# Weight and token sums on VectorE, squares on ScalarE, and another order of the first down tile

## The chip, the cores and the metric

The kernel runs on one core of a Trainium2 chip. The metric is the device time of one execution in microseconds (us), the median of the runs. Names of engines in the rows: PE is TensorE (PEld its weight loads), DVE is VectorE, ACT is ScalarE, POOL is GpSimd, SP is SyncE, which here only issues DMAs.

## What is computed

One layer of an encoder, for 2048 prompt tokens and 64 sample tokens: a token mixer (attention, a state space model, a short convolution) and then a feed-forward part. The change lies in the feed-forward part, with D = 1024 and D_FF = 4096:

```python
x += W_down relu(W_up rmsnorm(x))^2
```

## The kernel before

**Stages.** The mixer with its projections takes about the first half of the time. It writes the normalized tokens h, transposed, to DRAM (h_d) and x to x2_d. Then comes the up stage (`phase_up`), which forms f = relu(W_up h)^2 and writes it to f_d, and then the down stage (`phase_down`), which reads f_d back and adds W_down f to x.

**Splits.** All matmuls are made of reduced-precision f32 operands: a value is split into a high half (ScalarE, a copy to the type fp32r) and a low half (VectorE, the value less its high half), and a product takes three matmuls, high·high, high·low, low·high.

**Up stage.** The 2112 tokens come in 3 blocks of 704, and a block is two halves of 352 (TH). d_ff comes in 16 groups of 256 columns. A *pair* is one group with one block: 48 pairs, numbered n = 16·b + f. A pair is a 2×2×2 block product (256 columns, 1024 inputs, 704 tokens, each cut in two) done with seven block products in place of eight, in the manner of Strassen and Winograd. For this it needs four sums of weight blocks, t1 to t4, for every pair, and four sums of token blocks, s1 to s4, for every block of tokens. Each of the seven products is 12 matmuls of 128x352 (4 slices of the inputs × 3 of the splits), 84 a pair. They stand in the list ORDER and are numbered 0 to 6: 11·11, s1·t1, s2·t2, s4·22, s3·t3, 12·21, 22·t4 (tokens·weights).

- `load_h(b)` (L1555) loads the tokens of a block to two tiles hr, from the GpSimd queue for block 0, else from SP's. `load_w(n)` (L1561) loads the weights of a pair to wr, which has two buffers.
- `tokens(b)` (L1563) forms s1 (L1579), s2 (L1581), s3 (L1582, in place in hr) and s4 (L1589) on GpSimd and splits all seven operands (L1574 on ScalarE, L1575 on VectorE). The sums s1, s2, s4 lie in tiles st with two buffers. In the rows the split tiles are as (from sums) and a.
- `weights(n)` (L1600) forms t1 to t4 on GpSimd (L1606 to L1609) in the tile tt, which has one buffer, and splits the seven weight operands (L1613, L1614) to tiles ws with ten buffers. In the rows they are wt (from sums) and w.
- `pair(b, f)` (L1646) runs the products (matmuls at L1643) into three PSUM banks, pa (products 0, 2, 4, 6, one on top of the other), pd (1, 3) and pb (5). Between them ScalarE copies pa to c11 after product 0 (L1657), pd to c22 (L1660) and pa to c12 after product 2 (L1663). VectorE adds: c12 += pd (L1666), c22 += pa after product 4 (L1670), c11 += pb (L1674); c21 is the relu of pa after product 6, on ScalarE (L1678). A product that adds to pa has to wait for the copy or addition that reads pa before it. VectorE squares each of the four quarters, 128x352, with relu (L1653), and SP stores the tile sm of 128x4x352 (L1680).
- `late_rows` (L1617) makes the last 128 prompt tokens' h during the first pairs.

**Down stage.** For each of 8 groups of four weight tiles (load L1718, split L1722 and L1723) and each of 17 token tiles, `tile` (L1751) does the products (L106 to L108) into PSUM and adds them to x (L1765); `load_f` (L1728) and `split_f` (L1743, L1744) bring the rows of f.

**Order.** The engines are not fed in the order of the source: a scheduler orders each engine's instructions by what they depend on, and each engine then works through its own list in order, waiting where an operand or a buffer isn't ready.

## Time and profile before

| | us |
|---|---|
| median of three runs | 2852.26 (2850.14 to 2855.62) |
| profiled execution, its own time | 2861.32 |
| its span in the trace | 2859.6 |
| TensorE busy in the span | 2701.5 (94%) |
| VectorE | 1808.2 (63%) |
| ScalarE | 1123.2 (39%) |
| GpSimd | 740.6 (26%) |

Times in the trace are counted from the start of the span. Busy times include the tail of an instruction that overlaps the next: matmuls are pipelined, so a dozen of 2.08 us starts 1.9 us after the dozen before it. The last matmul of the stage ahead of the up stage ends at 1412.47 us, the up stage's last at 2119.62, and the down stage's first starts at 2128.41. The mean granted clock of TensorE in the span is 0.972 of full speed.

### The profile page before, as it was taken

To read this page: it belongs to the slowest core of one execution; us is meant where nothing else is said; L and a number is where in the kernel's file an instruction comes from. 1 tells how busy PE (TensorE), PEld (TensorE's weight loads), DVE (VectorE), ACT (ScalarE), POOL (GpSimd) and SP (SyncE) were. 2 spreads that over 40 slices of the span, in tenths; PEclk is the share of its full clock that TensorE was granted. 3 is DMA by queue.
4 is the path that set the end of the run, shared out by engine and by line. 5 is a ranking of instruction groups with operands and counts; after the bars stand their busy time and mean duration, and the time that the engine had idled before them with its cause. 6 is when DMAs were issued, how large, how long until landed. Compare 5 with 4: busy or idle time off the path is not lost.

```text
span 2859.6 us, 39208 instructions
## 1 busy us (share of the span) xinstructions
PE 2701.5 (94%) x14438; PEld 2344.2 (82%) x14438; DVE 1808.2 (63%) x3367; ACT 1123.2 (39%) x2239; POOL 740.6 (26%) x770
## 2 busy tenths in 40 slices
PE   7999999788789999999889989999989999999999
PEld 7999998655556776688689979989988888888887
DVE  7647478478455677577678888888864444434433
ACT  5424243155557678833343444444431111111110
POOL 2101014122742225422345454444410000000000
PEclk9999999889899999999999999999999999999999
DMA  7545555533644134375435344333454222222223
GB/s 221 181 120 161 159 126 176 103 82 83 105 78 116 46 93 125 103 212 168 161 127 162 135 140 138 126 120 130 135 189 155 76 81 76 68 58 76 52 71 121
DMA packets 365715, 347.14 MB, mean 121 GB/s; under 512 B 43342, under 2 KB 324254, under 8 KB 362542
## 3 DMA queue, kind: packets, MB, share of 16 engines
q1 hardware_dynamic: 362707, 335.53, 40.7%
q0 software_dynamic: 2816, 9.11, 1.0%
q8 instruction: 114, 1.87, 0.3%
q14 instruction: 78, 0.64, 0.1%
HBM read 237.05 MB, written 107.46 MB: 120 GB/s over the span
## 4 chain that ended last, share of the span: by engine, by line
PE 46%; DVE 2%; POOL 1%; issue 1%; ACT 0%; DMA 0%; SPq 0%; DVEq 0%; ACTq 0%; POOLq 0%
PE pa L1643 12%; PE pd L106 8%; PE pd L107 8%; PE pd L108 8%; PE pd L1643 6%; PE pb L1643 3%; PE pd L114 1%; PE pd L113 1%; DVE sm L1653 0%; DVE wt L1614 0%; POOL s L1589 0%; DVE as L1575 0%; DVE w L1614 0%; DMA fr<-f_d 0%; POOL tt L1607 0%
## 5 line engine op out<-in xcount | busy, mean ns | idle before, releaser
L1765 DVE TENSOR_TENSOR acc<-acc,pd 128x512 f32<-128x512 f32 x272 | 186.7, 686 | 419.5 <-PE pd L108 414.2
L106 PE MATMUL pd<-dw,fh 128*128 128x512 f32 x1024 | 398.9, 390 | 8.8 <-ACT dw L1722 8.8
L107 PE MATMUL pd<-dw,fh 128*128 128x512 f32 x1024 | 399.0, 390 | 0.0
L108 PE MATMUL pd<-dw,fl 128*128 128x512 f32 x1024 | 398.6, 389 | 0.0
L1743 ACT ACTIVATE fh<-fr 128x512 fp32r<-128x512 f32 x128 | 81.0, 633 | 547.5 <-PE pd L107 537.8
L1250 DVE TENSOR_TENSOR pl<-p,ph 128x512 fp32r<-128x512 f32 (+2 forms) x242 | 176.2, 744 | 117.8 <-ACT ph L1249 107.9
L1151 DVE TENSOR_REDUCE pm<-mx 128x1 f32<-128x512 f32 (+2 forms) x320 | 185.3, 606 | 78.5 <-PE mx L1146 52.5
L106 PEld LDWEIGHTS pd<-dw,fh 128*128 128x128 f32 x1024 | 192.5, 188 | 49.0 <-ACT dw L1722 9.1
L107 PEld LDWEIGHTS pd<-dw,fh 128*128 128x128 f32 x1024 | 192.5, 188 | 41.2 <-DVE dw L1723 1.4
L108 PEld LDWEIGHTS pd<-dw,fl 128*128 128x128 f32 x1024 | 192.4, 188 | 39.9
L1246 ACT ACTIVATE p<-st 128x512 f32<-128x512 f32 (+2 forms) x320 | 165.8, 545 | 96.4 <-PE st L1242 51.9
L1643 PE MATMUL pa<-as,wt 128*128 128x352 f32 x1152 | 201.0, 323 | 0.0
L1613 ACT ACTIVATE wt<-tt 128x512 fp32r<-128x512 f32 x192 | 121.1, 631 | 173.6 <-PE pb L1643 51.7
L1643 PEld LDWEIGHTS pa<-as,wt 128*128 128x128 f32 x1152 | 188.1, 190 | 1.0 <-ACT sm L1657 0.5
L1614 DVE TENSOR_TENSOR wt<-tt,wt 128x512 fp32r<-128x512 f32 x192 | 184.1, 960 | 7.0 <-ACT wt L1613 2.6
L1614 DVE TENSOR_TENSOR w<-wr,w 128x512 fp32r<-128x512 f32 x144 | 154.2, 1071 | 49.9 <-ACT w L1613 49.8
L106 PE MATMUL pq<-wh,xh 128*128 128x384 f32 (+1 forms) x512 | 179.9, 351 | 5.0 <-ACT xh L233 4.6
L108 PE MATMUL pq<-wh,xl 128*128 128x384 f32 (+1 forms) x512 | 174.8, 341 | 0.5 <-DVE xl L234 0.3
L1249 ACT ACTIVATE ph<-p 128x512 fp32r<-128x512 f32 (+2 forms) x320 | 174.1, 582 | 2.1
L107 PE MATMUL pq<-wl,xh 128*128 128x384 f32 (+1 forms) x512 | 174.7, 341 | 0.0
L1250 POOL TENSOR_TENSOR pl<-p,ph 128x512 fp32r<-128x512 f32 (+1 forms) x78 | 95.0, 1221 | 255.2 <-ACT ph L1249 183.2
L1606 POOL TENSOR_TENSOR tt<-wr 128x512 f32<-128x512 f32 x48 | 68.5, 1427 | 343.5 <-DVE wt L1614 324.8
(483 smaller groups left out, 6403.7 us busy)
## 6 DMA issues: line engine op xcount, KB each, us to landing
wr<-in_w_up_dram SPq DMA_DIRECT2D x46, 1024.0 KB
f_d<-sm SPq DMA_DIRECT2D x48, 704.0 KB
fr<-f_d SPq DMA_DIRECT2D x128, 256.0 KB
raw<-in_w_in_dram SPq DMA_DIRECT2D x51, 512.0 KB
dr<-in_w_down_dram SPq DMA_DIRECT2D x28, 512.0 KB
qk_d<-stgT SPq DMA_DIRECT2D x16, 768.0 KB
xt<-in_x_prompt_dram SPq DMA_DIRECT2D x16, 512.0 KB
ka<-qk_d SPq DMA_DIRECT2D x16, 512.0 KB
```

The source lines that it names most:

```text
L106: nc.tensor.matmul(out, lh, rh, start=first, stop=False)
L107: nc.tensor.matmul(out, lh, rl, start=False, stop=False)
L108: nc.tensor.matmul(out, ll, rh, start=False, stop=last)
L1151: nc.vector.tensor_reduce(pm[:, t, c:c + 1], p[:, :n], axis=AX.X, op=ALU.max)
L1246: nc.scalar.activation(p[:, c0:], st[:, c0:], AF.Exp)
L1249: nc.scalar.activation(ph[:, c0:], p[:, c0:], AF.Copy)
L1250: (nc.gpsimd if g.idle and j else nc.vector).tensor_tensor(pl[:, c0:], p[:, c0:], f32(ph)[:, c0:], op=ALU.subtract)
L1613: ac.activation(t[:, 0], src[nm], AF.Copy)
L1614: ve.tensor_tensor(t[:, 1], src[nm], f32(t)[:, 0], op=ALU.subtract)
L1643: nc.tensor.matmul(bank, w[:, x, k], a[:, y, k], start=first and k + j == 0, stop=k + j == 5, skip_group_check=not first)
L1743: nc.scalar.activation(h, r, AF.Copy)
L1765: nc.vector.tensor_tensor(a[:, o], a[:, o], p, op=ALU.add)
```

## The change

- **Token sums.** `sums(b)` is split off `tokens(b)`: s1, s2, s4 and s3 are formed on VectorE, and the tiles st have three buffers. It is stepped, one sum a product, from the pair f = 13 of the block before, in the source; the loads of the tokens are asked for at f = 10 in place of 12.
- **Weight sums.** t1 to t4 are formed on VectorE for every pair but the first, which stays on GpSimd. `load_w(1)` stands after the weights and tokens of pair 0.
- **Squares.** The four squares on VectorE go. In their place ScalarE does a relu over c12 and c22 together (128x704), a relu over c11 (128x352), and one square of the whole tile (128x1408), in place.
- **First down tile.** In the first of the tiles of the down stage both halves of the outputs are done for one weight tile before the next one; the splits of the first token tile stand behind two of the four weight splits in the source.

```diff
-    def tokens(b):
+    def sums(b):
         h0, h1 = hr[b]
         a11, a12, a21, a22 = h0[:, 0:4], h0[:, 4:8], h1[:, 0:4], h1[:, 4:8]
...
-            return up.tile([128, 4, TH], F32, tag="st", bufs=2, name=f"{nm}_{b}")
...
-        po.tensor_tensor(s1, a21, a22, op=ALU.add)
...
-        po.tensor_tensor(s2, s1, a11, op=ALU.subtract)
-        po.tensor_tensor(a21, a11, a21, op=ALU.subtract)
...
+        s1, s2, s4 = (up.tile([128, 4, TH], F32, tag="st", bufs=3, name=f"{x}_{b}") for x in ("s1", "s2", "s4"))
+        src[b] = {"11": a11, "s1": s1, "s2": s2, "s4": s4, "s3": a21, "12": a12, "22": a22}
+        ve.tensor_tensor(s1, a21, a22, op=ALU.add)
         yield
+        ve.tensor_tensor(s2, s1, a11, op=ALU.subtract)
         yield
-        po.tensor_tensor(s4, a12, s2, op=ALU.subtract)
+        ve.tensor_tensor(s4, a12, s2, op=ALU.subtract)
         yield
+        ve.tensor_tensor(a21, a11, a21, op=ALU.subtract)
         yield
+    def tokens(b):
+        for i, (nm, _) in enumerate(ORDER):
+            t = A[b, nm] = up.tile([128, 2, 4, TH], F32R, tag=f"a{i}", name=f"a{nm}_{b}")
+            ac.activation(t[:, 0], src[b][nm], AF.Copy)
+            ve.tensor_tensor(t[:, 1], src[b][nm], f32(t)[:, 0], op=ALU.subtract)
+            yield
...
-        po.tensor_tensor(t1, b12, b11, op=ALU.subtract)
...
+        eng = po if n == 0 else ve
+        eng.tensor_tensor(t1, b12, b11, op=ALU.subtract)
+        eng.tensor_tensor(t2, b22, t1, op=ALU.subtract)
+        eng.tensor_tensor(t3, b22, b12, op=ALU.subtract)
+        eng.tensor_tensor(t4, b21, t2, op=ALU.subtract)
...
-        def square(c):
-            ve.scalar_tensor_tensor(c, c, 0.0, c, op0=ALU.max, op1=ALU.mult)
...
         ac.activation(c21, pa, AF.Relu)
-        square(c21)
+        r = sm[:, 2:4]
+        ac.activation(r, r, AF.Relu)
+        ac.activation(c11, c11, AF.Relu)
+        ac.activation(sm, sm, AF.Square)
...
     load_h(0, nc.gpsimd)
+    for _ in sums(0):
+        pass
     load_w(0, nc.gpsimd)
-    load_w(1, nc.gpsimd)
     weights(0)
     for _ in tokens(0):
         pass
+    load_w(1, nc.gpsimd)
...
-            if b < 2 and f == NP2 - 4:
+            if b < 2 and f == NP2 - 6:
                 load_h(b + 1)
             if n + 1 < 3 * NP2:
                 weights(n + 1)
-            nxt = tokens(b + 1) if b < 2 and f == NP2 - 1 else iter(())
+            if b < 2 and f == NP2 - 3:
+                nxt = sums(b + 1)
+            if b < 2 and f == NP2 - 1:
+                nxt = tokens(b + 1)
             pair(b, f, lambda: next(nxt, None))
...
+        if q + t == 0:
+            for j in range(QF):
+                for hf in range(2):
+                    products(hf, j)
         for hf in range(2):
-            o = slice(hf * 512, hf * 512 + 512)
-            p = ps.tile([128, 512], F32, tag="dn", bufs=6, name=f"pd{q}_{t}_{hf}")
-            for j in range(QF):
...
+            p, o = pp[hf], slice(hf * 512, hf * 512 + 512)
+            if q + t:
+                for j in range(QF):
+                    products(hf, j)
```

How the lists of the engines change, at three places. A name like w22_12 is the weight operand 22 of pair 12; the last number of a name only tells tiles apart.

**ScalarE, from pair 11 to 12 before.** The relu of c21 of a pair stands between the weight splits for the pair after the next, and the copy of c11 of the next pair (L1657) three rows on.

```order
L1613 ACTIVATE w11_13_16899<-wr13_16758 128x512
L1613 ACTIVATE wt1_13_16902<-tt13_16894 128x512
L1678 ACTIVATE sm11_16789<-pa11_16786 128x352
L1613 ACTIVATE wt2_13_16905<-tt13_16894 128x512
L1613 ACTIVATE w22_13_16908<-wr13_16758 128x512
L1657 ACTIVATE sm12_16923<-pa12_16920 128x352
L1613 ACTIVATE wt3_13_16911<-tt13_16894 128x512
```

The same stretch one pair sooner, after the change. The three new instructions of pair 10 are L1661, L1662 and L1663; the copy of c11 of pair 11 is L1641.

```order
L1661 ACTIVATE sm10_16657<-sm10_16657 128x704
L1600 ACTIVATE wt1_12_16763<-tt12_16755 128x512
L1662 ACTIVATE sm10_16657<-sm10_16657 128x352
L1659 ACTIVATE sm10_16657<-pa10_16654 128x352
L1600 ACTIVATE wt2_12_16766<-tt12_16755 128x512
L1663 ACTIVATE sm10_16657<-sm10_16657 128x1408
L1600 ACTIVATE w22_12_16769<-wr12_16620 128x512
L1641 ACTIVATE sm11_16784<-pa11_16781 128x352
```

The square over 1408 columns now stands ahead of one weight split and of the copy of c11.

**VectorE, in pair 8 before.** sm8 is the output tile of pair 8; L1666 and L1670 are the additions to c12 and c22.

```order
L1614 TENSOR_TENSOR w22_9_16390<-wr9_16246,w22_9_16390 128x512
L1614 TENSOR_TENSOR wt3_9_16393<-tt9_16376,wt3_9_16393 128x512
L1614 TENSOR_TENSOR w21_9_16396<-wr9_16246,w21_9_16396 128x512
L1666 TENSOR_TENSOR sm8_16405<-pd8_16403,sm8_16405 128x352
L1653 SCALAR_TENSOR_TENSOR sm8_16405<-sm8_16405 128x352
L1614 TENSOR_TENSOR wt4_9_16399<-tt9_16376,wt4_9_16399 128x512
L1670 TENSOR_TENSOR sm8_16405<-pa8_16402,sm8_16405 128x352
```

The same stretch of VectorE after: L1569, L1571 and L1573 are s1, s2 and s4 of block 1, L1650 and L1653 the additions.

```order
L1601 TENSOR_TENSOR w22_9_16382<-wr9_16239,w22_9_16382 128x512
L1569 TENSOR_TENSOR s1_1_17051<-hr1_1_16623 128x1408
L1601 TENSOR_TENSOR wt3_9_16385<-tt9_16368,wt3_9_16385 128x512
L1571 TENSOR_TENSOR s2_1_17052<-s1_1_17051,hr1_0_16622 128x1408
L1601 TENSOR_TENSOR w21_9_16388<-wr9_16239,w21_9_16388 128x512
L1650 TENSOR_TENSOR sm8_16397<-pd8_16395,sm8_16397 128x352
L1601 TENSOR_TENSOR wt4_9_16391<-tt9_16368,wt4_9_16391 128x512
L1573 TENSOR_TENSOR s4_1_17053<-hr1_0_16622,s2_1_17052 128x1408
L1653 TENSOR_TENSOR sm8_16397<-pa8_16394,sm8_16397 128x352
```

The scheduler has put three sums of block 1, whose pairs start with 16, into pair 8, ahead of its addition to c22; the first waits for the loads of hr1_1. The squares are gone.

**GpSimd, at the start of the up stage before.** The first rows are the loads of the weights of pair 1 and the sums of pair 0.

```order
L1561 DMA wr1_15264<-in_w_up_dram 128x8x256
L1606 TENSOR_TENSOR tt0_15266<-wr0_15262 128x512
L1608 TENSOR_TENSOR tt0_15266<-wr0_15262 128x512
L1607 TENSOR_TENSOR tt0_15266<-wr0_15262,tt0_15266 128x512
L1579 TENSOR_TENSOR s1_0_15292<-hr0_1_15257 128x1408
L1609 TENSOR_TENSOR tt0_15266<-wr0_15262,tt0_15266 128x512
L1581 TENSOR_TENSOR s2_0_15294<-s1_0_15292,hr0_0_15256 128x1408
L1582 TENSOR_TENSOR hr0_1_15257<-hr0_0_15256,hr0_1_15257 128x1408
```

After, from the load of the weights of pair 0:

```order
L1561 DMA wr0_15269<-in_w_up_dram 128x8x256
L1561 DMA wr1_15318<-in_w_up_dram 128x8x256
L1593 TENSOR_TENSOR tt0_15271<-wr0_15269 128x512
L1595 TENSOR_TENSOR tt0_15271<-wr0_15269 128x512
L1594 TENSOR_TENSOR tt0_15271<-wr0_15269,tt0_15271 128x512
L1596 TENSOR_TENSOR tt0_15271<-wr0_15269,tt0_15271 128x512
```

The load for pair 1 still stands ahead of the four sums of pair 0, though the source has it behind them; before it waited for nothing late, after it waits for VectorE's and TensorE's last use of a buffer of the stage ahead. The token sums are no longer in this list.

## Rows read from the trace of the kernel before

**Rows 1.** Busy time by stretch: us, then busy (instructions) by engine, PEclk, DMA share, GB/s

```profile
1412.47:2119.62 707.15, 659.47 (x4041) 655.29 (x4040) 580.22 (x699) 311.93 (x555) 332.46 (x204) 0.96 0.39 132
1412.47:1457.71 45.24, 23.82 (x107) 22.28 (x107) 31.58 (x35) 21.62 (x33) 27.48 (x12) 0.74 0.29 93
1915.00:2119.00 204.00, 204.00 (x1286) 203.89 (x1285) 163.19 (x210) 85.67 (x159) 86.11 (x60) 1.00 0.39 131
```

**Rows 2.** Waits from 1400 to 2125: us in total, times, longest

```profile
POOL tt L1606 <- DVE wt L1614: 324.8, 44, 13.6
...
PE pa L1643 <- DVE sm L1670: 27.7, 5, 7.1
```

**Rows 3.** Timeline of PE: start, us, group [idle before <-releaser]

```profile
1445.17 0.95 PE L1643 MATMUL pb<-a,w 128*128 128x352 f32 x2 [6.02 <-ACT w L1613]
...
1548.72 2.08 PE L1643 MATMUL pa<-a,w 128*128 128x352 f32 x12
...
1565.99 3.89 PE L1643 MATMUL pa<-a,wt 128*128 128x352 f32 x12 [5.58 <-DVE sm L1670]
1569.67 3.11 PE L1643 MATMUL pa<-a,w 128*128 128x352 f32 x12
...
1673.42 3.89 PE L1643 MATMUL pa<-a,wt 128*128 128x352 f32 x12 [7.07 <-DVE sm L1670]
...
1705.61 3.48 PE L1643 MATMUL pa<-a,wt 128*128 128x352 f32 x12 [6.61 <-DVE sm L1670]
...
1905.07 3.89 PE L1643 MATMUL pa<-a,wt 128*128 128x352 f32 x12 [6.99 <-DVE sm L1670]
```

**Rows 4.** Timeline of POOL, at the start, in pair 8, at the first block seam

```profile
1412.24 1.26 POOL L1609 TENSOR_TENSOR tt<-wr,tt 128x512 f32<-128x512 f32 x1
...
1416.59 4.55 POOL L1582 TENSOR_TENSOR hr<-hr,hr 128x1408 f32<-128x1408 f32 x1
...
1554.72 3.23 POOL L1579 TENSOR_TENSOR s<-hr 128x1408 f32<-128x1408 f32 x1 [3.66 <-DMA hr<-h_d]
...
1561.52 3.43 POOL L1582 TENSOR_TENSOR hr<-hr,hr 128x1408 f32<-128x1408 f32 x1
...
1659.10 5.74 POOL L1589 TENSOR_TENSOR s<-hr,s 128x1408 f32<-128x1408 f32 x1 [5.94 <-DVE as L1575]
```

**Rows 5.** Timeline of DVE, at the same three places

```profile
1414.50 9.66 DVE L1575 TENSOR_TENSOR a<-hr,a 128x1408 fp32r<-128x1408 f32 x3 [2.11 <-ACT a L1574]
...
1443.07 1.62 DVE L1575 TENSOR_TENSOR as<-s,as 128x1408 fp32r<-128x1408 f32 x1 [9.49 <-ACT as L1574]
1444.62 1.29 DVE L1614 TENSOR_TENSOR wt<-tt,wt 128x512 fp32r<-128x512 f32 x2
...
1553.43 0.69 DVE L1614 TENSOR_TENSOR wt<-tt,wt 128x512 fp32r<-128x512 f32 x1 [0.18 <-ACT wt L1613]
...
1561.87 3.63 DVE L1614 TENSOR_TENSOR wt<-tt,wt 128x512 fp32r<-128x512 f32 x1
...
1666.29 2.52 DVE L1575 TENSOR_TENSOR as<-s,as 128x1408 fp32r<-128x1408 f32 x1 [4.09 <-ACT as L1574]
```

**Rows 6.** Groups by shape, 1400 to 2125: count | busy us, mean ns | idle before

```profile
L1614 DVE TENSOR_TENSOR wt<-tt,wt 128x512 fp32r<-128x512 f32 x192 | 184.1, 960 | 7.0 <-ACT wt L1613 2.6
...
L1653 DVE SCALAR_TENSOR_TENSOR sm<-sm 128x352 f32<-128x352 f32 x192 | 152.2, 794 | 7.1 <-ACT sm L1678 2.6
L1613 ACT ACTIVATE wt<-tt 128x512 fp32r<-128x512 f32 x192 | 121.1, 631 | 173.6 <-PE pb L1643 51.7 <-issue 44.0 <-PE pd L1643 38.9
...
L1670 DVE TENSOR_TENSOR sm<-pa,sm 128x352 f32<-128x352 f32 x48 | 25.1, 523 | 7.5 <-PE pa L1643 7.3
...
L1574 ACT ACTIVATE as<-s 128x1408 fp32r<-128x1408 f32 x9 | 12.3, 1372 | 15.4 <-POOL s L1589 15.4
```

**Rows 7.** Timeline of ACT: the copy of c11 in pair 8

```profile
1551.38 0.45 ACT L1657 ACTIVATE sm<-pa 128x352 f32<-128x352 f32 x1
```

**Rows 8.** Timeline of DVE: the last square of the up stage

```profile
2120.14 0.53 DVE L1653 SCALAR_TENSOR_TENSOR sm<-sm 128x352 f32<-128x352 f32 x1 [1.32 <-ACT sm L1678]
```

More of the change, by code (lines that the diff above doesn't have):

```diff
@@ L1666, in pair @@
         ve.tensor_tensor(c12, pd, c12, op=ALU.add)
-        square(c12)
         product(b, n, 4, pa, False)
@@ L1670, in pair @@
         ve.tensor_tensor(c22, pa, c22, op=ALU.add)
-        square(c22)
         product(b, n, 5, pb, True)
@@ L1674, in pair @@
         ve.tensor_tensor(c11, pb, c11, op=ALU.add)
-        square(c11)
         product(b, n, 6, pa, False)
@@ L1688, in phase_up @@
         pass
+    load_w(1, nc.gpsimd)
     late = late_rows()
     NP2 = NF // 2
+    nxt = iter(())
     for b in range(3):
@@ L1755, in tile, with products @@
         last = q == NF // QF - 1
-        for hf in range(2):
-            o = slice(hf * 512, hf * 512 + 512)
-            p = ps.tile([128, 512], F32, tag="dn", bufs=6, name=f"pd{q}_{t}_{hf}")
-            for j in range(QF):
-                w = wts[q * QF + j]
-                if t < 16:
-                    mm3(nc, p, h[:, j], l[:, j], w[:, 0, o], w[:, 1, o], j == 0, j == QF - 1)
-                else:
-                    mm2(nc, p, h[:, j], w[:, 0, o], w[:, 1, o], j == 0, j == QF - 1)
+        pp = [ps.tile([128, 512], F32, tag="dn", bufs=6, name=f"pd{q}_{t}_{hf}") for hf in range(2)]
+        def products(hf, j):
+            p, w, o = pp[hf], wts[q * QF + j], slice(hf * 512, hf * 512 + 512)
+            if t < 16:
+                mm3(nc, p, h[:, j], l[:, j], w[:, 0, o], w[:, 1, o], j == 0, j == QF - 1)
+            else:
+                mm2(nc, p, h[:, j], w[:, 0, o], w[:, 1, o], j == 0, j == QF - 1)
+        if q + t == 0:
+            for j in range(QF):
+                for hf in range(2):
+                    products(hf, j)
+        for hf in range(2):
+            p, o = pp[hf], slice(hf * 512, hf * 512 + 512)
+            if q + t:
+                for j in range(QF):
+                    products(hf, j)
             nc.vector.tensor_tensor(a[:, o], a[:, o], p, op=ALU.add)
@@ L1778, in phase_down @@
         load_w(f, nc.gpsimd)
-    for f in range(QF):
+    for f in range(2):
         split_w(f)
-    for i in range(3):
-        load_f(*work[i])
+    load_f(*work[0])
+    split_f(*work[0])
+    for f in range(2, QF):
+        split_w(f)
+    load_f(*work[1])
+    load_f(*work[2])
     load_x(0)
     load_x(1)
-    split_f(*work[0])
     for i, (q, t) in enumerate(work):
```

27 lines of the change are left out of this document (2 added, 25 removed).

## The prediction

> **What bounds the kernel now.** Start with the stages. The up stage runs from the last matmul of the stage before it, at 1412.47 us, to the end of its own last matmul at 2119.62: 707.15 us, in which TensorE is busy 659.47 us at a mean granted clock of 0.96 [rows 1]. Undisturbed, as in its last 204 us, TensorE has no gap at all, the clock is 1.00, and a matmul takes 204.00 / 1286 = 0.1586 us [rows 1]. The stage has 48 pairs × 84 = 4032 matmuls, which is 639.5 us at that pace. So 67.6 us are lost, and nothing that leaves the matmuls alone can gain more here. A pair takes 84 × 0.1586 = 13.3 us.
>
> Where are they lost? The waits say that after the first pairs TensorE waits for one thing only: the addition at L1670 (c22) on VectorE, 27.7 us in 5 waits [rows 2]; product 6 of a pair may add to pa only after that addition has read it. The timeline has the four long ones: 5.58, 7.07, 6.61 and 6.99 us, **26.25 us** in all [rows 3]. After each the engine runs slower. At 1565.99 the granted clock has dropped and the next two dozens take 3.89 and 3.11 us instead of 2.08, which is 2.84 us more; the first dozens after the others take 3.89, 3.48 and 3.89, so 1.81 + 1.40 + 1.81 more [rows 3]. The **clock** costs at least 7.9 us; I take 8. The **start** is the rest: up to 1457.71, 45.24 us go by for 107 matmuls, which are worth 17.0 us [rows 1], so 28.3 us are lost there. 26.25 + 8 + 28.3 = 62.5 of the 67.6.
>
> Why is the addition late? At 1565.99 and 1705.61 it is GpSimd's three token sums, back to back (3.23 to 3.43 us each), and a low-half split beside them on VectorE takes 3.63 us where it takes 0.69 alone [rows 4, 5]. At 1673.42 and 1905.07, the block seams, it is s4: it has to wait 5.94 us for a buffer, since st has two, and takes 5.74 us; ScalarE and then VectorE wait for it, VectorE 4.09 us, with the addition queued behind [rows 4, 5].
>
> **The change, part by part.**
>
> *Weight sums from GpSimd to VectorE.* Before, a pair costs VectorE seven low halves at about 0.96 us, four squares at 0.79 and three additions at 0.52: 11.5 of 13.3 us [rows 6]. The first two means are swollen by GpSimd's work beside them; alone a half takes 0.69 [rows 5]. After it, seven halves and four sums at 0.69 and three additions at 0.52 make 9.2 us. In the middle of the stage this is worth nothing, since TensorE doesn't wait there; it makes the room for what follows. GpSimd itself waits 324.8 us for VectorE [rows 2], so its removal frees nothing by itself.
>
> *Squares from VectorE to ScalarE.* ScalarE gets a relu over 704 columns, one over 352 and a square over 1408 a pair. Nearest row: L1574, 128x1408, 1.372 us, against 0.631 for 512 [rows 6]; that is 0.83 ns a column, so 0.79 + 0.50 + 1.37 = 2.7 us. With 7 × 0.63 + 4 × 0.46 = 6.3 before, ScalarE is then busy 9.0 of 13.3 us. What counts is the order: the square stands ahead of one weight split and the copy of c11, which must have read pa before product 2 writes it, two products (3.81 us) into the pair. Before, the copy ends 2.66 + 0.45 = 3.11 us after the pair's first matmul [rows 3, 7]; laid out by its order with these durations it ends at about 3.4 us. Some 0.4 us is left, so the cost is nothing; if the square took twice as long it would not be (rival D).
>
> *Token sums ahead of their block, on VectorE, st with three buffers.* This removes GpSimd's back-to-back sums and the wait at the seam: 26.25 us of stalls and 8 of clock go. It adds three waits. VectorE is now the engine that waits for the tokens of block 1: s1 stands in pair 8, behind the fourth split for pair 9. There, GpSimd waited 3.66 us for the same transfer, which was in at 1554.72, 6.0 us after the pair's start at 1548.72 [rows 3, 4]. From 6.0, VectorE does s1, a split, s2, a split, the c12 addition, a split, s4 and the c22 addition: 3 × 1.54 + 3 × 0.60 + 2 × 0.5 = 7.4, so c22 is ready at 13.4 us and product 6 wanted it at 11.4 (6 × 1.905): a stall of **2.0 us**, 0 if the transfer comes 2 us sooner. Block 2 has the same in pair 17; its transfers are issued after other work of the seam, and I put 0 to 3 us there, value 1.2. The clock after these: 0.1 to 2.8 us each, value 0.7. At the two seams I lay out VectorE's list with 1.54 us for each of the splits, and c22 comes 0.2 us ahead of its need; 0 to 2 us in all, value 0.5.
>
> *The start.* VectorE's list from 1414.50 becomes: seven large operations (three splits, four sums), seven weight halves, four large splits. In a row one large operation starts 1.55 us after another and two halves take 1.29 [rows 5], so 1.54 and 0.60 us each, and the list ends at 1435.7. But GpSimd's four sums for pair 0 now run beside it: the next load of weights stands before them in GpSimd's queue, and it waits for the buffer that the stage before frees at its end. What such a company costs is seen at the same place before: three splits took 9.66 us instead of 4.8, while GpSimd did its own [rows 4, 5]. Four sums at 1.26 us [rows 4] in between give 1440.8. TensorE then has some 74 matmuls done about 6 us later, after low-clock dozens, so its lost time is 17.7 to 22.7 us instead of 28.3. What went: VectorE's wait of 9.49 us for s4 through ScalarE at 1443.07 [rows 5], and with it TensorE's wait of 6.02 us at 1445.17 [rows 3]. Gain 5.6 to 10.6, value **7**.
> The Trainium skill ("SBUF — State Buffer", section "SBUF: two separate sides") has GpSimd and a VectorE operation with two SBUF inputs exclude each other for a whole instruction. By that rule the start is the late end, a gain of 5.6, and without it 10.6; the trace agrees, 9.66 us for three splits, and so I stay near the late one.
>
> *First down tile.* TensorE takes the weight tiles in the order in which they are split; the other engines keep their order there. Worth 0.4 us at most, as a few of the tile's matmuls are left behind the last split. The last square of the stage now takes 1.37 instead of 0.53 us [rows 6, 8] ahead of its store and of the loads that TensorE waits for: +0.8. Together +0.4.
>
> **The sum.** 26.25 + 8 + 7 = 41.2 gained; 2.0 + 1.2 + 1.4 + 0.5 + 0.4 = 5.5 given back: 35.7. The profiled execution took 2861.3 us, so 2825.6; it stood 9.1 us above the median of 2852.26, and on the median it is 2816.6. I say **2816**.
>
> **The rivals.**
> A, the forecast, 2808 to 2824. For it: each stall has one cause in the rows, and the change removes each cause.
> B, *the wait moves to VectorE*: the transfers of tokens land late, VectorE stands with its whole list behind s1, and the stalls of pairs 8 and 17 are 5 us each with 2 us of clock. 14 instead of 4.6 given back: about 2826. For it: GpSimd did wait for this transfer; against: it never waited over 3.7 us.
> C, *the start gains nothing*, because it is as long with GpSimd's late sums: 2824. For it: the first stage of VectorE's list has grown from three to seven large operations; against: the 9.49 us behind s4 are gone for certain.
> D, *ScalarE is late for c11*. In-place Square over 1408 columns has no row; its floor is 1.37 us, and were it twice that, the copy of c11 would end at 4.8 instead of 3.4 and TensorE would wait 1.0 us in 46 pairs: 46 us, a time of 2862, slower than before. It decides from 0.78 us a pair (35.7 / 46); below that it only eats the gain, and 0.2 us a pair gives 2825. For it: no row shows this operation, the slack is only 0.4 us, and it is asked for 46 times; against: ScalarE's rows, 352, 512 and 1408 columns, lie on one line of 0.83 ns a column [rows 6, 7].
> The Trainium skill ("ScalarE: Activation LUTs", section "Rules for kernel authors") speaks against this part: relu and multiplications belong on VectorE. Its case is a faster bf16 mode; here in f32 the rows have 1.372 us for 1408 columns on ScalarE and 0.53 for 352 on VectorE, so it would cost some 0.6 us of an engine's spare time a pair, and no run here shows more.
> E, *the change does nothing*, because TensorE bounds the steady pairs anyway: within 5 us of 2852. Against it: the stalls are in the rows.
>
> **How the numbers follow.** A 0.66, B 0.13, C 0.11, D 0.07 (0.03 of it slower than before, 0.01 within 0.2%), E 0.03. The range reaches from A's good end, with all new waits at nothing (2816 - 5 - 4 = 2807, and 2 for what my 62.5 leaves out), to B with C and the small D: **2805 to 2832**. A difference of 0.2%, 5.7 us, is about what can be told from no change: faster 0.94, within 0.2% 0.03, slower 0.03.
>
> **What would show it.** After: no wait of TensorE for the c22 addition above 3 us; granted clock at or near 1.00 from 1460 to the end of the stage, and the stage about 671 us long. Low halves at 0.69 us on the mean. A wait of VectorE for the transfer of hr in pairs 8 and 17. The lost time of the start near 21 us. It is wrong if TensorE waits in every pair for the copy of c11 (D), or if the start still takes 28 us (C).

## The result, and the profile after

The changed kernel takes **2813.63 us** (median of 4 runs, 2809.31 to 2824.33), the kernel before, on the same chip, 2853.94 (4 runs, 2850.14 to 2865.24). The ratio is 0.9858, with an interval of 0.9817 to 0.9899, so 40 us less, 29 to 52. It was forecast at 2816, with a range of 2805 to 2832. The profiled execution took 2809.31 us.

Read the stages first. These are busy times by stretch of the kernel after; columns as in [rows 1]: us, busy (instructions) of PE, PEld, DVE, ACT, POOL, then PEclk, DMA share, GB/s. The rows are the up stage, its first 45.24 us (as long a stretch as the one in [rows 1]), its middle without the start, 460 us of that without any wait, and last the stage with the gap to the first matmul of the down stage.

```profile
1394.42:2065.68 671.26, 654.88 (x4041) 651.67 (x4040) 460.17 (x709) 418.08 (x698) 8.73 (x9) 0.99 0.42 140
1394.42:1439.66 45.24, 30.38 (x168) 29.15 (x168) 41.46 (x50) 29.42 (x47) 6.56 (x5) 0.81 0.46 145
1440.00:2060.00 620.00, 618.48 (x3839) 616.78 (x3838) 415.89 (x657) 387.08 (x649) 2.17 (x4) 1.00 0.42 141
1600.00:2060.00 460.00, 460.00 (x2853) 459.10 (x2853) 309.04 (x484) 290.80 (x483) 2.17 (x4) 1.00 0.41 138
1394.42:2075.28 680.86, 654.90 (x4041) 651.67 (x4040) 461.57 (x712) 422.17 (x704) 8.73 (x9) 0.98 0.42 142
```

The up stage is 707.15 - 671.26 = 35.9 us shorter, and 35.1 with the gap behind it, which was 715.94 - 707.15 = 8.8 and is 9.6. The granted clock is 1.00 behind the start. The spans differ by 2859.6 - 2807.6 = 52.0 us; of this 1412.47 - 1394.42 = 18.1 lie ahead of the up stage, where both kernels have the same code. That part is not counted to the change: in the fourteen profiles of this study that stage ends between 1394 and 1429 us, and for the kernels that were profiled twice at 1394 and 1405, at 1408 and 1409, at 1403 and 1414. (Of the 1429, 7.55 us do belong to an edit; they are told under *token sums back on GpSimd*.) One of its waits shows why. TensorE's matmuls of L1078 wait for tiles loaded from the key cache, for this long in all between 600 and 1000 us (us, times, longest), after:

```profile
PE sa_pk L1078 <- DMA sa_y<-in_cache_k_dram: 2.9, 2, 2.7
```

In the kernel before it was 13.8 us, and 9.7 when the changed kernel was profiled a second time. So single spans are not compared below; **U** is, the time from the last matmul ahead of the up stage to the first of the down stage: 715.94 before, 680.86 after.

The waits from 1400 to 2085 us, after (us in total, times, longest):

```profile
PE pa L1630 <- ACT w L1600: 11.7, 1, 11.7
...
PE pa L1630 <- DVE sm L1653: 1.5, 1, 1.5
...
DVE s L1569 <- DMA hr<-h_d: 2.2, 1, 2.2
```

Against [rows 2], TensorE's 27.7 us in 5 waits for the addition to c22 (now L1653) are down to a single 1.5. The timeline of PE shows it in its place (start, us, group, idle before):

```profile
1521.98 2.07 PE L1630 MATMUL pa<-a,w 128*128 128x352 f32 x12
...
1535.27 2.19 PE L1630 MATMUL pa<-a,wt 128*128 128x352 f32 x12 [1.52 <-DVE sm L1653]
1537.30 1.94 PE L1630 MATMUL pa<-a,w 128*128 128x352 f32 x11
```

1521.98 is the start of pair 8. The work behind the wait isn't slow, 2.19 us for a dozen where [rows 3] had 3.89 and 3.11: this short wait cost no clock. VectorE's timeline has the reason for the wait, and the state of the start:

```profile
1396.45 6.11 DVE L1583 TENSOR_TENSOR a<-hr,a 128x1408 fp32r<-128x1408 f32 x2 [2.12 <-ACT a L1582]
...
1527.84 1.62 DVE L1569 TENSOR_TENSOR s<-hr 128x1408 f32<-128x1408 f32 x1 [2.17 <-DMA hr<-h_d]
...
1533.16 1.62 DVE L1573 TENSOR_TENSOR s<-hr,s 128x1408 f32<-128x1408 f32 x1
1534.69 0.52 DVE L1653 TENSOR_TENSOR sm<-pa,sm 128x352 f32<-128x352 f32 x1
```

VectorE stood 2.17 us for the tokens of block 1 in front of s1; the addition came right behind s4. At the start two splits took 6.11 us beside GpSimd's weight sums. These stood behind the load of wr1 in GpSimd's list, which waited for TensorE's last use of the buffer in the stage ahead; and ScalarE's copy of c11 in pair 8 comes early enough:

```profile
1393.85 0.88 POOL L1561 DMA_DIRECT2D wr<-in_w_up_dram  x1 [20.21 <-PE po L108]
...
1524.85 0.45 ACT L1641 ACTIVATE sm<-pa 128x352 f32<-128x352 f32 x1
```

Groups by shape from 1400 to 2085 us, after (count | busy us, mean ns | idle before):

```profile
L1601 DVE TENSOR_TENSOR wt<-tt,wt 128x512 fp32r<-128x512 f32 x192 | 131.6, 689 | 71.4 <-ACT wt L1600 68.1
...
L1663 ACT ACTIVATE sm<-sm 128x1408 f32<-128x1408 f32 x48 | 66.0, 1375 | 0.1
...
L1661 ACT ACTIVATE sm<-sm 128x704 f32<-128x704 f32 x48 | 38.1, 794 | 32.4 <-DVE sm L1653 32.2
L1593 DVE TENSOR_TENSOR tt<-wr 128x512 f32<-128x512 f32 x47 | 32.4, 689 | 1.3
```

Low halves are at 689 ns (960 in [rows 6]), the square takes 1375 ns, the relu 794.

### The profile page after: what moved, and what is told of

It is laid out like the page before. It is cut to its first block, busy times and chain, and to the rows that moved or that the text cites. A ratio compares the mean times of both kernels' runs of the same rounds, so it can differ in the third digit from the quotient of the medians.

```text
span 2807.6 us, 38902 instructions
## 1 busy us (share of the span) xinstructions
PE 2689.5 (96%) x14438; PEld 2335.1 (83%) x14438; DVE 1692.3 (60%) x3375; ACT 1231.5 (44%) x2383; POOL 409.5 (15%) x570
## 3 DMA queue, kind: packets, MB, share of 16 engines
q0 software_dynamic: 2816, 9.11, 1.0%
## 4 chain that ended last, share of the span: by engine, by line
PE 83%; DMA 5%; DVE 4%; ACT 3%; issue 2%; POOL 2%; SPq 1%; DVEq 0%; ACTq 0%; POOLq 0%
PE pa L1630 13%; PE pd L106 8%; PE pd L107 8%; PE pd L108 8%; PE pd L1630 6%; PE pb L1630 3%; PE pq L108 2%; PE pq L106 2%; PE pq L107 2%; PE mx L1146 2%; PE st L1237 2%; PE po L106 2%; PE st L1238 2%; PE po L1258 2%; PE po L107 2%
## 5 line engine op out<-in xcount | busy, mean ns | idle before, releaser
L1601 DVE TENSOR_TENSOR wt<-tt,wt 128x512 fp32r<-128x512 f32 x192 | 131.6, 689 | 71.4 <-ACT wt L1600 68.1
L1601 DVE TENSOR_TENSOR w<-wr,w 128x512 fp32r<-128x512 f32 x144 | 99.1, 688 | 91.5 <-ACT w L1600 91.4
L1237 PE MATMUL st<-q,kb 67*128 67x512 f32 (+2 forms) x320 | 129.5, 406 | 22.1 <-DMA q<-m_d 12.3
L1600 ACT ACTIVATE w<-wr 128x512 fp32r<-128x512 f32 x144 | 90.3, 627 | 92.6 <-PE pa L1630 92.6
```

What stands on the lines that cost most here:

```text
L1237: nc.tensor.matmul(st[:, c0:], kb[i][:, kc], q1[i][:, q0 + c0:q0 + 512], start=True, stop=False)
L1600: ac.activation(t[:, 0], src[nm], AF.Copy)
L1601: ve.tensor_tensor(t[:, 1], src[nm], f32(t)[:, 0], op=ALU.subtract)
```

## The experiments

The theory: the four long stalls came from the token sums on GpSimd, so the token sums on VectorE, ahead of their block, are the part that pays, with some of the start. Rivals: the *room*, that the sums only fit on VectorE because the squares left it; and the *weight sums*, that the weight sums on GpSimd beside VectorE's work were the cause, whoever does the token sums. Besides, one thing in the trace after was not forecast and wanted a cause: the **pace**. 460 us for 2853 matmuls are 161.2 ns each; before they took 158.6 in [rows 1]. Ratios in this section are against the kernel before on the same chip, at 2861.17, 2860.41, 2859.62 or 2858.39 us.

**Squares back on VectorE.** The rest is as in the changed kernel.

```diff
+        def square(c):
+            ve.scalar_tensor_tensor(c, c, 0.0, c, op0=ALU.max, op1=ALU.mult)
...
-        r = sm[:, 2:4]
-        ac.activation(r, r, AF.Relu)
-        ac.activation(c11, c11, AF.Relu)
-        ac.activation(sm, sm, AF.Square)
+        square(c21)
```

with square(c12), square(c22) and square(c11) behind their additions.

> The changed kernel with the four squares back on VectorE, the rest as changed. Theory of the prediction: VectorE then has 9.2 + 2.1 = 11.3 us of work in a pair of 13.3, so no pair waits; only the short wait in pair 8 grows from 1.5 to some 2 us. Time as the changed kernel's, 2809 to 2822. Rival: the squares' move made the room, then the waits for the c22 addition in pairs 8 and 17 and at the block seams are 3 us and more again, 2825 to 2840. On the pace of the matmuls (161.1 ns apart in the changed kernel, 158.9 in the one before, both at full clock): if ScalarE's new work slows them, 158.9 here; if the place of the tiles does (a third st buffer), or the missing work of GpSimd, 161.1.

Measured: 2818.78 us, a ratio of 0.9842 (0.9815 to 0.987). U of this kernel (stretch, us, busy and counts):

```profile
1413.31:2086.37 673.06, 649.39 (x4041) 646.68 (x4040) 540.34 (x904) 310.07 (x560) 8.74 (x9) 0.98 0.43 143
```

U is 673.06, which is 7.8 us *less* than in the changed kernel, and behind the start TensorE has no wait at all. In pair 8 the scheduler has put the addition to c22 ahead of s4, where it takes its usual time:

```profile
1550.27 0.52 DVE L1658 TENSOR_TENSOR sm<-pa,sm 128x352 f32<-128x352 f32 x1
```

So the room wasn't needed, and that rival falls: the squares on ScalarE show no gain in this change. Of the 7.8 us 0.8 are the gap to the down stage, 1.5 the wait in pair 8, and most of the rest the pace, 460 us for 2878 matmuls, 159.8 ns. The wait and the pace are not shown to be the squares' doing: the wait doesn't come in a second execution of the changed kernel, and the pace can differ between two executions of one program (both below). The times, 0.9842 against 0.9858, don't tell the two kernels apart.

**Weight sums back on GpSimd.** `eng = po if n == 0 else ve` becomes `eng = po`.

> The changed kernel with the weight sums of all pairs on GpSimd, the rest as changed. Theory of the prediction: steady pairs don't wait; next to the token sums on VectorE, GpSimd's four sums of 1.3 to 1.7 us hold it up, so the wait in pair 8 grows from 1.5 to 4 us, one of 2 to 4 us appears in pair 17 and 1 to 3 us at each seam, with 1.5 us of clock each: 2820 to 2835. Rival: their move adds nothing, since TensorE is the bound, 2809 to 2820. On the pace of the matmuls: 158.9 ns if work on GpSimd is what the changed kernel lacks; 161.1 if it is ScalarE's squares or the place of the tiles.

Measured: 2837.82 us, 0.9918 (0.989 to 0.9946), a little above what was expected. U, and TensorE's waits from 1400 to 2130 us:

```profile
1414.44:2109.64 695.20, 654.81 (x4041) 649.25 (x4040) 442.84 (x524) 419.16 (x704) 300.32 (x197) 0.98 0.42 139
```

```profile
PE pd L1630 <- ACT wt L1600: 7.5, 2, 5.3
PE pa L1630 <- ACT sm L1641: 5.5, 4, 2.1
PE pa L1630 <- DVE sm L1653: 5.2, 4, 1.7
```

U is 14.3 us longer than in the changed kernel. 7.3 of these are in the start, where 122 matmuls are done in 45.24 us instead of 168 (46 × 0.1586). The sums for pair 1 now stand on GpSimd, and TensorE has to wait 5.3 us for their splits. The stalls in pairs 8 and 17 and at the seams are short, 1.7 us at most: with the token sums on VectorE the long ones don't come back. Behind each of them TensorE waits once more, 0.7 to 2.1 us, for ScalarE's copy of c11 (L1641): this is rival D's wait, and it comes where ScalarE itself is held up: behind the stall in pair 8, a weight split that stands ahead of the square had waited 2.31 us for GpSimd's sums. So the weight sums on GpSimd alone were not the cause of the long stalls.

**Token sums back on GpSimd**, formed with their splits during the pair ahead of their block, as before, with two buffers; the loads of tokens again at f = 12, and the sums of block 0 on GpSimd too.

```diff
-    for _ in sums(0):
-        pass
...
-            if b < 2 and f == NP2 - 3:
-                nxt = sums(b + 1)
```

> The changed kernel with the token sums as they were (on GpSimd, at the seam, two st buffers), weight sums on VectorE and squares on ScalarE as changed. Theory of the prediction: the two waits at the block seams stay at 4 to 7 us with 2 us of clock, since they come from the missing buffer and GpSimd's 5.7 us for s4; the waits in pairs 8 and 17 shrink to 0 to 3 us, since VectorE has 9 instead of 11.5 us of work; the start is between the two kernels: 2828 to 2842. Rival: without weight sums GpSimd is in time and nothing waits, 2809 to 2820. On the pace of the matmuls: 158.9 ns if the third st buffer is what slows them, 161.1 if it is ScalarE's squares or the lack of GpSimd's work.

Measured: 2850.51 us, 0.9958 (0.9939 to 0.9976): most of the gain is gone. U, and the wait for the c22 addition (L1667 here):

```profile
1429.07:2125.62 696.55, 661.08 (x4041) 655.86 (x4040) 467.05 (x703) 422.21 (x703) 33.68 (x13) 0.97 0.41 137
```

```profile
PE pa L1644 <- DVE sm L1667: 16.3, 4, 6.2
```

The four stalls are back, at 6.22, 1.99, 6.01 and 2.05 us. The place was expected the wrong way round: the long ones are in pairs 8 and 17, and the two at the seams are short. At the seams GpSimd, rid of the weight sums, now has s4 done in 3.65 us where [rows 4] had 5.74. In pair 8 three token sums stand back to back on GpSimd whatever else it does, and the weight sums, now on VectorE, are held up beside them. VectorE and GpSimd there:

```profile
1561.88 3.25 DVE L1615 TENSOR_TENSOR wt<-tt,wt 128x512 fp32r<-128x512 f32 x1
1565.16 3.52 DVE L1607 TENSOR_TENSOR tt<-wr 128x512 f32<-128x512 f32 x1
1568.61 0.68 DVE L1609 TENSOR_TENSOR tt<-wr 128x512 f32<-128x512 f32 x1
```

```profile
1561.05 3.53 POOL L1581 TENSOR_TENSOR s<-s,hr 128x1408 f32<-128x1408 f32 x1
1564.54 3.60 POOL L1582 TENSOR_TENSOR hr<-hr,hr 128x1408 f32<-128x1408 f32 x1
```

A VectorE operation of 0.68 us takes about 3.5 us, as long as a GpSimd operation runs, and is back at 0.68 when the last has ended, at 1568.14. The Trainium skill ("SBUF — State Buffer", section "SBUF: two separate sides") has the two engines lock each other out for an instruction; these rows agree.

At the start, the token sums of block 0 on GpSimd reach ahead of U. They fall on the last normalization of the stage ahead; VectorE, then TensorE:

```profile
1412.58 12.13 DVE L128 TENSOR_TENSOR rm_h<-rm_h,rt_h 128x1 f32<-128x1 f32 x1
```

```profile
1427.13 1.94 PE L1488 MATMUL pht<-ident,hs 128*128 128x128 f32 x8 [7.55 <-DVE hs L1480]
```

This operation, 0.16 us in the kernel before, lasts until GpSimd has issued a load and done six sums without a break, to 1424.70, and TensorE waits 7.55 us just before U begins. Inside U the start then has 196 matmuls in 45.24 us against 168 in the changed kernel, 28 × 0.1586 = 4.4 us more; with the 7.55 it is 3.1 us worse. In the same way U's gain over the kernel before, 715.94 - 696.55 = 19.4 us, is 11.8 with the 7.55, and that fits the times, 10.7 us below 2861.17.

**The third buffer alone**, in the kernel before: `bufs=2` of the tiles st becomes `bufs=3`.

> The kernel before with a third buffer for the token sums and nothing else. Theory of the prediction: at the two block seams s4 no longer waits 5.9 us for a buffer, so the waits of 7 us there fall to 0 to 2 with their clock, and the start loses part of its 28 us; those in pairs 8 and 17 stay: 2832 to 2842. Rival: s4 with its 5.7 us on GpSimd is late anyway, within 4 us of the kernel before. On the pace of the matmuls: 161.1 ns if the place of the tiles sets it, 158.9 if not.

Measured: 2857.31 us, 0.9984 (0.9969 to 0.9999), less than 0.2%, where 2832 to 2842 was expected. PE at the first seam and in pair 17, and GpSimd in pair 8:

```profile
1671.66 3.54 PE L1643 MATMUL pa<-a,wt 128*128 128x352 f32 x12 [2.92 <-DVE sm L1670]
...
1705.83 2.42 PE L1643 MATMUL pa<-a,wt 128*128 128x352 f32 x7 [8.98 <-DVE sm L1670]
```

```profile
1566.85 3.63 POOL L1589 TENSOR_TENSOR s<-hr,s 128x1408 f32<-128x1408 f32 x1
```

At the seams the buffer did most of what was expected: 7.07 became 2.92, where 0 to 2 was expected. But s4, which had waited for the buffer, now follows the three other sums as a fourth in a row in pairs 8 and 17, and the stall there grows from 6.61 to 8.98 in pair 17. The start lost 30.8 us, 91 matmuls in 45.24 us, where before lost 28.3. A wait taken away on the engine that does the harm moved the harm.

**Token sums alone**, without the weight sums and the squares: `eng = po`, and the squares as in the first experiment. The later load of wr1 and the order of the first down tile stay in.

> Of the change only the token sums (on VectorE, ahead of their block, three buffers), the later load of pair 1's weights and the first down tile; weight sums on GpSimd and squares on VectorE as before. From the last matmul ahead of the up stage to the first of the down stage the kernel before takes 715.9 us, the changed one 680.9, and 673.1 with the squares back on VectorE. Theory of the prediction: the waits at the seams go, but VectorE has 11.5 us a pair with GpSimd beside it, so adding 8 large operations near the seams and 4 in pairs 8 and 17 makes the c22 addition 2 to 5 us late in four or more places, with clock: 695 to 712. Rival (the weight sums' move is not needed): 673 to 685.

Measured, in one execution: 2839.0 us.

```profile
1412.74:2105.04 692.30, 657.17 (x4042) 653.06 (x4041) 583.03 (x716) 314.83 (x560) 301.62 (x197) 0.97 0.42 139
```

```profile
PE pd L1630 <- ACT wt L1600: 7.4, 2, 5.3
PE pa L1630 <- DVE sm L1658: 6.2, 3, 2.8
```

U is 692.30, a little below the 695 to 708 expected. So the parts of the change, each added to the one ahead, as differences of single executions: token sums 715.94 - 692.30 = **23.6 us**; then the weight sums 692.30 - 673.06 = **19.2**, of which 46 × 0.1586 = 7.3 lie in the start (122 against 168 matmuls again) and most of the rest in the waits at the seams (2.8 us each, with slow dozens behind them); then the squares 673.06 - 680.86 = **-7.8**. The pace differs in these executions (in *token sums alone* block 1 stood at 161.1 ns, most of the rest at 158.9), so each difference is uncertain by several us; of the -7.8 some 5.5 are pace. No part alone does it all.

**A longer ScalarE step**, to price rival D: one more copy of the tile in place ahead of the square, which leaves the result as it is.

```diff
         ac.activation(c11, c11, AF.Relu)
+        ac.activation(sm, sm, AF.Copy)
         ac.activation(sm, sm, AF.Square)
```

> The changed kernel with ScalarE's pass over the output tile done twice: a copy in place over 1408 columns (1.37 us) ahead of the square, which leaves the result the same. This is the price of rival D. The order changes with it: the copy of c11 now stands ahead of both passes, but the copy of c22, which product 3 waits for 5.7 us into the pair, stands behind them. Theory of the prediction (ScalarE has only some 0.4 us to spare ahead of a copy that TensorE waits for): with its list counted from the c11 copy at 2.0 us, c22 is copied at about 7.1, so TensorE waits 1.0 to 1.5 us for ScalarE in most pairs, 46 to 70 us in all: 2860 to 2885. Rival (what counts is busy time, 10.4 of 13.3 us, and the copies' buffers give the rest): no wait in steady pairs, 2809 to 2825.

Measured, in one execution: 2834.31 us, where 2860 to 2885 was expected. U:

```profile
1404.49:2100.56 696.07, 665.81 (x4042) 649.70 (x4041) 455.51 (x712) 474.29 (x752) 8.74 (x9) 0.98 0.42 139
```

That is 15.2 us more than in the changed kernel, 1.4 of it in the gap behind the stage, and TensorE still hardly waits: 0.9 us in all for the copy of c11, though the work of ScalarE went from 422.17 to 474.29 us. The rival had taken the order as fixed. The scheduler gave TensorE another one: product 5 ahead of product 3, and the first product of the next pair in pieces. PE where pair 8 ends, a piece of pair 9's first product and then product 6 of pair 8:

```profile
1545.36 0.99 PE L1630 MATMUL pa<-a,w 128*128 128x352 f32 x5
...
1546.18 2.15 PE L1630 MATMUL pa<-a,wt 128*128 128x352 f32 x12
```

The other seven of that dozen stand elsewhere. A dozen behind a break takes 2.15 to 2.19 us instead of 2.07, about 0.1 us; with some three breaks a pair in 46 pairs that is 14 us, an estimate. Added up over the timeline behind the start, against the changed kernel, the broken rows cost about 13 us (86 dozens that start over 1.96 us before what follows them against 10, and 152 pieces of dozens against 26), waits with slow matmuls behind them 6 (2.7 of them for ScalarE's splits of tokens at the seams), the gap 1.4, and the spacing of the whole dozens, narrower in this execution, gave some 5.6 back. The price of this late ScalarE is thus 15 us, some 20 without the narrower spacing, against D's 46, and two thirds of it are paid in broken rows.

**One transpose more**, whose result nothing uses, behind pair 8, to see whether a break in the row of matmuls changes their pace.

```diff
+        if n == 8:
+            lt = ps.tile([128, 4, 128], F32, tag="lt", bufs=2, name="extra_p")
+            nc.tensor.transpose(lt[:, 0, :], sm[:, 0, :128], g.ident)
```

> The changed kernel with one transpose more (128x128, its result unused) on TensorE in pair 9, whose cost is 0.1 us. It tests what sets the distance of the matmuls at full clock, 158.9, 160.0 or 161.1 ns in the runs so far. Theory now: it is a matter of how the matmuls and weight loads stand to each other, set anew by each break in the row, and kept until the next; so the step is another after the transpose (158.9 or 160.0) up to the block seam, and up to 2.2 ns x 550 matmuls = 1.2 us are gained there. Rivals: the place of the tiles or the other engines' work sets it: 161.1 ns before and behind the transpose.

Measured, in one execution: 2817.83 us, U 681.84. PE around it:

```profile
1543.69 2.19 PE L1630 MATMUL pa<-a,wt 128*128 128x352 f32 x12 [1.93 <-DVE sm L1653]
...
1548.23 0.33 PE L1666 MATMUL extra_p<-ident,sm 128*128 128x128 f32 x1
...
1549.69 2.09 PE L1630 MATMUL pa<-as,wt 128*128 128x352 f32 x12
```

Ahead of the wait in pair 8 the dozens start 1.907 us apart (158.9 ns); the matmuls between the wait and the transpose are already about 161 ns apart, and behind it they stay at 161.1. Nothing follows for the pace, except that not every break changes it.

**Start and squares**: squares on VectorE, and the loads and sums of pair 0's weights ahead of the token sums of block 0.

```diff
     load_h(0, nc.gpsimd)
-    for _ in sums(0):
-        pass
     load_w(0, nc.gpsimd)
+    load_w(1, nc.gpsimd)
     weights(0)
+    for _ in sums(0):
+        pass
     for _ in tokens(0):
         pass
-    load_w(1, nc.gpsimd)
```

> The changed kernel with the squares on VectorE, and at the start both weight loads and the weight sums of pair 0 ahead of the token sums. The load for pair 1 then no longer waits for the end of the stage ahead, GpSimd's four sums are done before VectorE's large splits, and seven weight halves stand ahead of one large sum. Theory of the prediction: the 3.0 us that two splits lost to GpSimd in the changed kernel (6.11 us instead of 3.1) are gone, and the first product starts 1 to 2 us sooner: from the last matmul ahead of the stage to the first of the down stage 668 to 671 us, against 673.1 with the start as changed. Rival: the start is bound by VectorE's list as a whole, whose length is the same: 672 to 674.

Measured: 2812.12 us, 0.983 (0.9797 to 0.9863). U, the first 45.24 us, and 180 us without a wait:

```profile
1407.82:2076.14 668.32, 648.61 (x4041) 644.83 (x4041) 537.02 (x904) 309.99 (x560) 2.17 (x4) 0.99 0.43 143
1407.82:1453.06 45.24, 34.28 (x194) 32.78 (x195) 43.21 (x59) 28.25 (x46) 0.00 (x0) 0.89 0.40 132
1880.00:2060.00 180.00, 180.00 (x1135) 180.00 (x1134) 132.14 (x234) 76.19 (x145) 0.00 (x0) 1.00 0.36 121
```

GpSimd is through with its sums ahead of this stretch (0.00 busy in it), and the same two splits take half the time:

```profile
1409.85 3.16 DVE L1583 TENSOR_TENSOR a<-hr,a 128x1408 fp32r<-128x1408 f32 x2 [2.11 <-ACT a L1582]
```

So the 6.11 us after were GpSimd's four sums beside VectorE. The later load of wr1, which the changed kernel's source puts behind, held them back; this experiment moves the sums and the load together. 194 against 168 matmuls is 4.1 us of the start, and U is at the low end of the 668 to 671 expected.

**The changed kernel again**, on a later chip, and beside it *start and squares* with the former order of the first down tile.

> The changed kernel again, on the same chip as the next one. All views so far put its gain into the up stage (707.1 to 671.3 us) and nothing into the stages ahead of it, which take 1394 to 1429 us by chance; so 0.985 to 0.989 of the kernel before, and 671 to 672 us again for the up stage. A rival would be that the earlier stages gained too, 0.982 or less.

> Token sums and weight sums on VectorE and the third buffer as changed; squares on VectorE as before; at the start the loads and weight sums of pair 0 ahead of the token sums; the first down tile as before. Theory: the up stage as with the same start and squares, 659.6 us against 671.3 in the changed kernel; the gap to the down stage 8.7 to 8.8; the first 24 matmuls of the down stage back at 7.4 to 7.7 us from 8.4 to 8.6. From the last matmul ahead of the up stage to the end 1400 us against 1413 in the changed kernel: 0.980 to 0.984 of the kernel before, 12 to 13 us less than the changed one. Rival: the order of the first down tile was worth something, then the down stage is longer with the old one.

Measured: the changed kernel 2819.31 us, 0.9853 (0.9829 to 0.9876), its up stage 670.31, a little under the 671 to 672 expected; the other 2815.72, 0.9847 (0.9821 to 0.9873), above the 0.980 to 0.984 expected. U and a stretch without a wait, of the changed kernel again, then of the other:

```profile
1404.62:2084.54 679.92, 655.38 (x4041) 652.23 (x4040) 461.54 (x712) 422.21 (x704) 8.73 (x9) 0.98 0.42 142
1610.00:2070.00 460.00, 460.00 (x2854) 459.07 (x2853) 308.91 (x483) 290.80 (x483) 2.17 (x4) 1.00 0.41 138
```

```profile
1402.82:2074.28 671.46, 651.71 (x4042) 648.35 (x4041) 537.67 (x904) 310.13 (x560) 2.17 (x4) 0.99 0.43 142
1875.00:2055.00 180.00, 180.00 (x1127) 180.00 (x1126) 133.89 (x237) 76.25 (x144) 0.00 (x0) 1.00 0.36 123
```

The changed kernel repeats within 1 us of U, and at the same pace (161.2 ns), this time without any wait for the addition to c22: VectorE waited 0.9 us in all for the tokens, where it had been 2.2. The other has TensorE's order of *start and squares* in the up stage, but U is 3.1 us longer: 180 / 1127 = 159.7 ns a matmul against 180 / 1135 = 158.6. Does the pace belong to the program, or to the execution?

**Both of the last versions again**, unchanged, to tell that.

> The kernel with the start and the squares on VectorE once more. Its matmuls stood 158.9, 160.0 and 158.9 ns apart in the blocks 0, 1 and 2 of tokens. If the spacing belongs to the program, the same three steps come again; if it is drawn by chance at each block seam, at least one block differs, and U is off 668.3 us by 1.5 us a step. A ratio of 0.981 to 0.985 in either case.

> The same kernel with the former order of the first down tile, once more: 160.0, 161.1 and 160.0 ns if the spacing belongs to the program, and U within 1 us of 671.5; other steps if it is chance.

Measured: *start and squares* 2812.34 us, 0.9834 (0.9814 to 0.9854); the one with the former order 2817.3 in one execution, U 670.01. U and 180 us of *start and squares* again:

```profile
1408.66:2079.21 670.55, 650.23 (x4042) 646.65 (x4041) 537.24 (x904) 310.18 (x560) 2.17 (x4) 0.99 0.43 142
1880.00:2060.00 180.00, 180.00 (x1127) 180.00 (x1126) 133.86 (x237) 76.24 (x144) 0.00 (x0) 1.00 0.37 123
```

The same program in the same stretch had 1135 matmuls the first time and 1127 now, and U is 2.2 us longer. In the blocks 1 and 2 its dozens start 160.0 × 12 ns apart in both, where it was 160.0 and 158.9 the first time; the other version went from 161.1 and 160.0 to 160.0 and 160.0. So the program alone does not set the pace, at least in these two kernels. The two executions of each ran on different chips, so whether the chip or chance chose the step isn't told apart; within one execution it changes from block to block.

U of *start and squares*, 668.3 and 670.6, is 9 to 13 us below the changed kernel's 680.9 and 679.9, and its ratios, 0.983 and 0.9834, are below 0.9858 and 0.9853, but all four intervals overlap. It is probably some microseconds better than the change: the traces show 4.1 in the start and 0.8 in the gap, which don't hang on the pace; the times don't prove it.

The order of the first down tile brings no gain that can be seen. From the first matmul of the down stage to the 25th it is 7.88 to 8.64 us in the ten profiles with the new order (8.55 and 7.94 in the changed kernel), and 7.42, 7.49, 7.70 and 8.56 in the four with the old one; if anything the new order is slower.

## Why the prediction was right, step by step

- **The stalls, 26.25 us: right.** All four are gone, and the experiments show whose they were. In pairs 8 and 17 it was GpSimd's token sums in a row, as forecast: they come back at 6.22 and 6.01 us when these sums alone go back to GpSimd. At the seams the forecast's cause, the missing buffer, was incomplete: the third buffer alone still left 2.9 us, the weight sums alone on GpSimd left 1.7 to 2.8, and the token sums alone on GpSimd with two buffers 2.0; only without either is there no wait.
- **The clock, 8 us: right.** From 1440 to 2060 us the mean granted clock is 1.00; it is below only at the start.
- **The wait that takes their place, 2.0 us in pair 8: right**, 1.52, by the path that was laid out: hr late, VectorE 2.17 us idle, c22 behind s4. It hangs on when the tokens land, as the prediction said: 1.93 us with the transpose, none when the changed kernel ran again. The 1.2 us for pair 17, the 0.5 for the seams and the 1.4 us of clock behind them did not come: 3.1 us of caution.
- **The start, 7 us (5.6 to 10.6): a little small.** Lost are 45.24 - 168 × 0.1586 = 18.6 us instead of 28.3, a gain of 9.7. The term that was too large is GpSimd's company: the two splits beside the four weight sums took 6.11 us where alone they take 3.16, so 3.0 us too many, and not the 5.1 (four sums of 1.26 us) that were put in. VectorE's list ended 26.2 us behind the stage's start, at 1420.59, which is the 23.2 of the prediction and 3.0; the rest is matmuls that TensorE did earlier than laid out. By the Trainium skill's rule of two engines that lock each other out ("SBUF — State Buffer", section "SBUF: two separate sides") it was to be the late end, 5.6; the direction agrees, the size is less, since not all four sums met a split (the first was through at 1396.03, the first split starts at 1396.45). The cause that was named, the end of the wait for s4, is only part of it: with the token sums alone on VectorE the start does 122 matmuls instead of 107, 2.4 us, and the other 7.3 came with pair 1's weight sums, which took TensorE 5.3 us of waiting as long as GpSimd did them.
- **The squares at no cost: right for the copy of c11; the rest is open.** The square takes 1.375 us (forecast 1.37), and the copy of c11 in pair 8 ends at 1524.85 + 0.45, 3.32 us behind the pair's start (forecast 3.4), half a microsecond ahead of its need. No wait. The first experiment has U 7.8 us shorter without this part. Of that, 0.8 is the last square, which was forecast, 1.5 a wait that didn't come again, and some 5.5 the pace, which no run ties to the squares.
- **The gap to the down stage, +0.4: +0.8.** The last square cost 0.8 as forecast; the 0.4 us for the order of the first tile did not come.
- **Not forecast: the pace.** 161.1 instead of 158.6 ns over the 3839 matmuls between 1440 and 2060: 620.00 - 1.52 - 3839 × 0.1586 = 9.6 us lost. It is the largest error in the working. The prediction took the 158.6 ns of 204 us of one profile for a constant of the kernel. (Some 1.2 of the 9.6 us are the yardstick: the dozens of that stretch start 158.9 × 12 ns apart, and a count of matmuls in a stretch includes those cut at its edges.)

Together: 26.25 + 8 + 9.7 - 1.5 - 9.6 = 32.9 us. The up stage gained 35.9; the 3.0 that are left are taken for part of the 5.1 us that the prediction's working leaves unplaced (67.6 - 62.5); no run places them. So the stage came out as forecast, 671.3 for about 671, because an unforeseen loss of 9.6 us was met by waits that were shorter or didn't come (0.5 + 3.1), a better start (2.7) and that rest (3.0). The terms of the stalls and of the clock were right, and they make the total; the closeness of the sum was luck.

The two comparisons of the changed kernel have 40 us, and the up stage with its gap 35. The 5 us are inside both intervals, and no run assigns them.

Of the rivals, B has the right mechanism at a tenth of its price. C fell, but *weight sums back on GpSimd* comes near it, with 45.24 - 122 × 0.1586 = 25.9 us lost at the start. D fell, since the square was no slower than its columns; its price for a late ScalarE was two to three times that of the longer step, 46 us against 15 to 20, because it held TensorE's order fixed. E fell.

## What to carry to other kernels

Where GpSimd and VectorE both work in SBUF, a row of large GpSimd operations stretched small VectorE operations beside it to their length, 0.68 to 3.5 us: look for the waiting engine's feeder in that state before blaming a buffer, because the third buffer alone only moved the stall. When the engine that bounds a stage has no waits left, its own pace is a term with an error of over a percent, and one stretch of one profile doesn't give it. Look ahead of the stage too: work moved to its start can hold up the end of the stage before it, outside the stretch that is compared. And price each part of a bundle by itself: here one part gave some 24 us, one some 19, and the third no gain that shows.

## What the runs showed of the hardware

Matmuls of 128x352 in an undisturbed row, at a granted clock of 1.00, come in three spacings: dozens start 1.907, 1.920 or 1.933 us apart, so 158.9, 160.0 or 161.1 ns a matmul. A spacing holds for up to hundreds of microseconds and changes at a break in the row: a split dozen, the transposes of `late_rows`, the wait in pair 8, a block seam. It can differ between two executions of the same program, on two chips, as the last runs show. Still, from pair 10 on it was 161.1 for nearly all the stage in all three profiles of the changed kernel (with the one that has a transpose more), and in nearly all of the kernel before it was 158.9. Whether squares on ScalarE make the slow step likelier is open: with the squares there and the weight sums on GpSimd, all three spacings occurred in one execution, 158.9 in the blocks 0 and 1 and 161.1 in block 2; and with the squares on VectorE 161.1 stood in block 1 of *token sums alone* and, once, of the version with the former order. A step of 1.1 ns over the stage's 4032 matmuls is 4.4 us, about as much as the times can tell apart.

A break in a row of matmuls without any wait costs about 0.1 us (2.15 to 2.19 us for the dozen behind it instead of 2.07), which is how a mere change of order cost about 13 us in the experiment with the longer ScalarE step.

A VectorE operation of one column, 0.16 us in the kernel before, lasted 12.13 us while GpSimd went through a load issue and six sums without a break (*token sums back on GpSimd*).
